# Attention's shared-out work dealt anew: one piece in the steps that weigh values and three in the others, and ten copies of weights in DRAM ahead of the attention instead of eight

## The chip, the cores and the metric

One NeuronCore of a Trainium2 chip runs the whole kernel. The metric is the device time of one execution in microseconds (us). Its engines work side by side, each through a queue of its own in a fixed order, and wait for each other through semaphores: PE (matmuls; PEld is its weight load), DVE (vector work), ACT (scalar activations and copies), POOL (GpSimd) and SP, which here only starts DMAs. POOL starts DMAs as well, among them all those that add into their destination.

## The reference, cut to what matters

One layer: attention over a sliding window, a residual, then a gated embedding. All in fp32.

```python
def swa_mixer(h, w_in, w_out, sinks, rel_bias):          # h: 512 x 2048
    q, k, v, gate = jnp.split(h @ w_in, ...)             # 32 q heads, 4 key/value heads, head size 64
    ...                                                  # blocks of 128; keys of this and the previous block
    scores = einsum(q, kb) * HD ** -0.5 + bias           # masked to a window of 128
    m = max(scores.max(-1), sink)
    e = exp(scores - m)
    probs = e / (e.sum(-1) + exp(sink - m))
    out = einsum(probs, vb)
    return (out * silu(gate)) @ w_out

def reference(...):
    x = x + swa_mixer(rmsnorm(x, norm_g), ...)
    x = x + (p @ ple_proj) * sigmoid(rmsnorm(x, ple_norm) @ ple_gate)
    return rmsnorm(x, final_g)
```

## The kernel before

Every fp32 matmul is three matmuls in a reduced format (`mm3`, L123 to L128): each operand is split into a high part and a rest, and high by high, high by rest and rest by high are added up in PSUM. The splitting is work for ACT (the high part is a cast) and DVE (the rest is a subtraction). For weights this is `W._make` (L104): it asks SP for the load after next, ACT makes `whi` (L109), DVE makes `wlo` (L110).

The stages follow each other on PE:

1. The first projections (k, v and two pieces of q) run while `first` is being loaded, up to about 71 us.
2. The other 30 pieces of the projections for q and the gate (`projections`, L856). A piece is 128 columns wide and takes 16 **k-steps** of three matmuls each. Half a piece needs one weight tile of 512 KB. The first 40 k-steps (L886) run alone, up to about 98 us.
3. The attention (loop L909) is woven into the rest of the projections: 64 **steps** i = 0 to 63, and three more in which its pipeline drains. Up to about 450 us. PE never has attention alone: each step holds 6 or 7 k-steps of projection.
4. The output projection and the embedding gate, in sub-products over sums of weights (seven instead of eight). The sums are made earlier: SP copies a block of weights from DRAM to DRAM (L693) and POOL adds another block onto the copy by a DMA (L695). There are 56 copies and as many adds. `sum_weights(n)` issues number n: an even n is a copy, an odd n the add for a copy that was issued seven numbers before.

One step i of the attention handles 32 queries of 8 heads. Several steps are in flight:

- `scores(i)`: PE multiplies q and k into `s` (L478; there is one such buffer). In the same step DVE adds the bias (`t`, L508) and takes the minimum (L511, into `sm`), ACT takes the exponential (L522) and, at the end of the step, DVE the reciprocal (L524). ACT scales the weights into `pr` (L533 to L537) in the next step.
- `turn(i-2)`: PE transposes `pr` into `pt` (L546), ACT casts the high part of `r` (L557), DVE subtracts the rest (L558); POOL masks a copy `own` (L565), of which ACT moves a half (L574).
- `weigh(i // 2 - 2)`, in even steps from 4 on: PE multiplies `r` by the values (L586, two matmuls, the second of which reads what L558 wrote) into `o`, one more matmul for `own` (L589), and then ACT copies halves of `o` into `tmp` (L598) and DVE adds them into `u` (L600).

PE's queue in a step begins with L586 (even steps), L546 and L478 and goes on with the step's k-steps. Between those, the rest is placed by hand in the loop L925: at each k-step n = 0 to 5 it calls parts of what is listed above and of these shared-out pieces:

- `W.todo` at n = 0: a weight tile's `whi` and `wlo`;
- `first_chores` at n = 0 and 4, up to step 5: splits of the values (`V`, L378, L379) and of their differences, and in steps 2 to 4 four DMAs each that spread the differences (L440);
- `chores`: three for each finished piece of projection. For q: `scaled` (DVE, L325), the high parts (ACT, L336), the rests (DVE, L334). For the gate: a product (DVE, L630), tanh (ACT, L631), a product (DVE, L624). A piece's PSUM bank is free after its third chore, and the piece after next is written into that bank;
- `idle`, if no chore is left: the splits of the next keys (L369, L367), the products of gate and output (L614).

Chores stand at n = 0, at n = 2 if more than one is left, and at n = 4, in every step alike. `weigh` goes on at n = 1 (L589) and n = 3 (L598, L600). At the end of a step come the copies and adds of weights that `sums_in(i)` lists. During the 40 k-steps ahead, eight copies are issued, at n = 6, 10, ..., 34 (L892); `SUMS_EARLY` counts the numbers that this covers.

Of the kernel before, what the change touches and what calls it, by code (L numbers as in the profile page):

```python
# [55 lines left out]
def trunk_kernel(ctx: ExitStack, tc: tile.TileContext, a: dict):  # L56
# [300 lines left out]
    def make_key(h):  # L357

        t, e = divmod(h, 2)
        k = K[h] = kvq.tile([P, S // QB, 2, QB], F32R, tag="k", name=f"k{h}", bufs=2)  # L360
        same = slice(64 * e, 64 * e + 64)

        def part(low):
            src = kt[t][same].rearrange("p (j k) -> p j k", k=QB)
            for o in (slice(0, 64), slice(64, 128)):
                if low:
                    nc.vector.tensor_sub(k[o, :, 1], src, k[same, :, 0].bitcast(F32))  # L367
                else:
                    nc.scalar.copy(k[o, :, 0], src)  # L369

        return partial_of(part, False), partial_of(part, True)
# [31 lines left out]
    for b in range(exact, BUCKETS):  # L403
        d = np.nonzero(bk == b)[0]
        if len(d):
            lo, n = P - 1 + int(d.min()), len(d)
# [35 lines left out]
    def first_chores(i, step):  # L442

        if step == 0 and i < NB - 1:
            make_diff(i + 1)
        if step and 1 <= i < NB:
            diffs[i][step - 1]()
        if step == 2 and 1 <= i - 1 < NB:
            spread_diff(i - 1)
        if step and 1 <= i - 2 < NB:  # L450
            split(V[i - 2], values[i - 2])[step - 1]()
# [87 lines left out]
    def turn(i):  # L539


        d, g = divmod(i, UNITS)
        pr = T.pop(i)
        pt = bank(f"pt{i}", "t")[:, :256]
        for u in range(2):
            nc.tensor.transpose(pt[:, u * P : (u + 1) * P], pr[:, u, :], ident)  # L546

        j, part = divmod(i, 2)
        if part == 0:
            own = None  # L550
            if g >= P // TQ:
                own = apool.tile([P, 2, S], F32R, tag="own", name=f"own{j}")
            PT[j] = apool.tile([P, 2, S], F32R, tag="r", name=f"r{j}"), own
        r, own = PT[j]
        rh, rl = (r[:, l].rearrange("p (h t u q) -> p t u h q", h=GROUP, t=2, u=2)[:, part] for l in range(2))
        src = pt.rearrange("p (u h q) -> p u h q", u=2, h=GROUP)
        nc.scalar.copy(rh, src)  # L557
        nc.vector.tensor_sub(rl, src, rh.bitcast(F32))  # L558
        yield
        b = j % 2  # L560
        flat = lambda v, rows: v[rows].rearrange("p l (h t q) -> p t (l h) q", h=GROUP, t=2)[:, part]
        if own is not None:
            rows = slice(0, P) if b else slice(0, HB)
            sign = -1 if b else 1
            nc.gpsimd.affine_select(  # L565
                out=flat(own, rows), in_=flat(r, rows).bitcast(F32), pattern=[[0, 2 * GROUP], [sign, TQ]],
                compare_op=ALU.is_ge, fill=0.0, base=(-HB - 1 if b else 0) + sign * part * TQ, channel_multiplier=-sign,
            )
        yield
        if own is not None:  # L570
            here, there = slice(HB, P), slice(0, HB)
            if not b:
                here, there = there, here
            nc.scalar.copy(flat(own, there)[:, :GROUP], flat(own, here)[:, GROUP:].bitcast(F32))  # L574

    def weigh(j):

        kv, m = divmod(j, S // HB)
        n, b = divmod(m, 2)
        r, own = PT.pop(j)  # L580
        if m == 0:
            U[kv] = apool.tile([P, 4, S], F32, tag="u", name=f"u{kv}", bufs=2)
        out = bank(f"o{j}", "o")
        first = V[0 if n == 0 else n - 1 + b][:, kv]
        for low in range(2):
            nc.tensor.matmul(out, first, r[:, low], start=low == 0, stop=own is None and low == 1)  # L586
        yield
        if own is not None:
            nc.tensor.matmul(  # L589
                out, DV[:, n - 1, b, kv * 2 * HD : (kv + 1) * 2 * HD], own[:, 0], start=False, stop=True  # L590
            )
        yield
        ops = out.rearrange("p (u e q) -> p u e q", u=4, e=2)
        dst = U[kv][:, :, m * HB : (m + 1) * HB]
        lower, upper = slice(0, 64), slice(64, 128)
        tmp = [apool.tile([P, 4, HB], F32, tag=f"tmp{e}", name=f"tmp{e}_{j}") for e in range(2)]
        for e, (o, x) in enumerate(((lower, upper), (upper, lower))):
            nc.scalar.copy(tmp[e][o], ops[x, :, e, :])  # L598
        for e, o in enumerate((lower, upper)):
            nc.vector.tensor_add(dst[o], ops[o, :, e, :], tmp[e][o])  # L600
        if m == S // HB - 1:
            for c in range(4 * kv, 4 * kv + 4):
                weighed.add(c)
                if c in open_gates:
                    idle.append(partial_of(gate_value, c))
# [3 lines left out]
    chores, idle = [], []  # L609
# [75 lines left out]
                copies.append((t, block(nm, *first, jj, m) if first else summed[nm, {6: 7, 4: 6}[p], jj, m]))  # L685
                adds.append((t, block(nm, *{7: (2, 2), 5: (1, 2), 6: (1, 1), 4: (2, 1)}[p], jj, m)))
    SUM_STEPS = 2 * len(copies) + 6
    SUMS_EARLY = 16

    def sum_weights(i):  # L690

        if i % 2 == 0 and i // 2 < len(copies):
            nc.sync.dma_start(*copies[i // 2])  # L693
        elif i % 2 == 1 and 0 <= i // 2 - 3 < len(adds):
            nc.gpsimd.dma_start(*adds[i // 2 - 3], accum_op=ALU.add, max_dma_last_dim=8192)  # L695
# [181 lines left out]
    def some(of, n=1):  # L877
        for _ in range(min(n, len(of))):
            of.pop(0)()
# [6 lines left out]
    for n in range(AHEAD):  # L886
        next(proj)
        if n % 4 == 3 and W.todo:
            W.todo.pop(0)()
        if n >= 2 * KC or n >= KC and n % 2:  # L890
            some(chores)
        if n >= 6 and n % 4 == 2 and n // 4 <= SUMS_EARLY // 2:  # L892
            sum_weights(2 * (n // 4 - 1))
    blocks = KVH * UNITS

    def sums_in(i):


        if i == 0:
            return ()  # L900
        if i < 4:
            return range(4 * i + 3, min(4 * i + 7, SUMS_EARLY), 2)
        n, of = SUM_STEPS - SUMS_EARLY, blocks - 4
        return range(SUMS_EARLY + (i - 4) * n // of, SUMS_EARLY + (i - 3) * n // of)

# [3 lines left out]
    for i in range(blocks + 3):  # L909

        before, softmax = softmax, scores(i) if i < blocks else iter(())
        turned = turn(i - 2) if 2 <= i < blocks + 2 else iter(())
        value = weigh(i // 2 - 2) if 4 <= i and i % 2 == 0 else iter(())
        next(value, None)
        next(turned, None)
        next(softmax, None)
        next(turned, None)
        next(before, None)
        next(softmax, None)
        first_chores(i, 0)  # L920
        if i in (6, 20, 36):
            idle.extend(make_key(1 + i // 16))
        todo = left // (blocks + 2 - i) if i < blocks + 2 else 0
        left -= todo
        for n in range(max(todo, 6)):  # L925
            if n < todo:
                next(proj)
            if n == 0:
                first_chores(i, 1)
                some(W.todo)  # L930
                some(chores or idle)
            elif n == 1:
                next(value, None)
            elif n == 2:
                if len(chores) > 1:
                    some(chores)
            elif n == 3:
                next(turned, None)
                next(value, None)
                next(softmax, None)  # L940
            elif n == 4:
                first_chores(i, 2)
                some(chores or idle)
            elif n == 5:
                next(softmax, None)
        if i < blocks:
            for n in sums_in(i):
                sum_weights(n)
# [434 lines left out]
    n = done[3]  # L1383
# [87 lines left out]
```

## Time and profile before

| | |
|---|---|
| runs, median | 797.51 us of 3 (797.0 to 798.45) |
| profiled execution | 797.58 us, of which 795.9 us are the span from its first to its last instruction |
| mean granted PE clock | 0.997 |
| PE busy | 783.1 us, 98% of the span |
| DVE, ACT, POOL busy | 590.7, 517.4, 141.7 us |
| HBM | 177.26 MB read, 62.97 MB written, 302 GB/s over the span |

The page gives for each engine how long it was busy. Since matmuls are pipelined, a record of one is longer (0.39 us) than the distance to the next start (0.23 us), so a short wait of PE hides in its busy time and is found in the starts of the timeline's rows instead. In the views, `[0.37 <-DVE sm L511]` behind an instruction is the idle time of its engine just before it and what ended that; a row of waits gives the total, the count and the longest, in us.

### The profile page before, as it was taken

The numbers are of one execution on the slowest core, as the hardware profiler recorded it, in microseconds if no ns is written. First come the engines' busy times: TensorE is split into PE (matmuls) and PEld (weight loads), VectorE is DVE, ScalarE is ACT, GpSimd is POOL, SyncE is SP. The second block draws the span as 40 slices with busy tenths as digits, with TensorE's granted clock in tenths as the row PEclk, the third lists the DMA queues.
The fourth block names the chain that finished last, engine by engine and source line by source line (L and its number), as shares of the span: only waits on it lengthen the run. The fifth ranks groups of instructions, "written<-read, shape, count | busy, mean of one in ns | idle before, by whom it ended". The sixth has DMA issues, their size and how long they took to land.

```text
span 795.9 us, 11177 instructions
## 1 busy us (share of the span) xinstructions
PE 783.1 (98%) x3658; PEld 649.4 (82%) x3658; DVE 590.7 (74%) x1171; ACT 517.4 (65%) x1131; POOL 141.7 (18%) x252
## 2 busy tenths in 40 slices
PE   9999999999999999999999999999999999999995
PEld 8888887878787888888888888888888888888885
DVE  4538567877887678776768799778867756988896
ACT  6635367876777667775767645456689656656765
POOL 0031122332243313341323100000000020210000
PEclk9999999999999999999999999999999999999998
DMA  9787779999899979889878498667873996796633
GB/s 349 231 227 262 204 181 283 296 237 285 242 254 260 249 227 249 240 235 274 241 201 181 126 367 317 224 208 233 286 243 127 348 201 201 162 230 208 190 106 106
DMA packets 44618, 184.87 MB, mean 232 GB/s; under 512 B 6720, under 2 KB 7232, under 8 KB 39440
## 3 DMA queue, kind: packets, MB, share of 16 engines
q1 hardware_dynamic: 36480, 142.94, 52.2%
q0 software_dynamic: 8080, 41.22, 27.4%
q8 instruction: 29, 0.48, 0.2%
q14 instruction: 29, 0.24, 0.1%
HBM read 177.26 MB, written 62.97 MB: 302 GB/s over the span
## 4 chain that ended last, share of the span: by engine, by line
PE 92%; DVE 4%; ACT 2%; DMA 1%; issue 1%; SPq 0%; ACTq 0%; DVEq 0%
PE gps L126 7%; PE gps L127 7%; PE gps L128 7%; PE qps L126 6%; PE qps L127 6%; PE qps L128 6%; PE g L128 5%; PE o L128 5%; PE g L127 5%; PE o L127 5%; PE o L126 5%; PE g L126 5%; PE vps L286 2%; PE s L478 2%; PE o L586 2%; PE pt L546 1%
## 5 line engine op out<-in xcount | busy, mean ns | idle before, releaser
L731 ACT CAST bhi<-braw 128x1024 fp32r<-128x1024 f32 x102 | 107.3, 1052 | 76.7 <-PE o L128 22.3
L732 DVE TENSOR_TENSOR blo<-braw,bhi 128x1024 fp32r<-128x1024 f32 x102 | 124.4, 1222 | 41.9 <-ACT bhi L731 41.5
L126 PE MATMUL gps<-xh,whi 128*128 128x512 f32 x256 | 100.5, 393 | 0.0
L127 PE MATMUL gps<-xl,whi 128*128 128x512 f32 x256 | 100.0, 391 | 0.0
L128 PE MATMUL gps<-xh,wlo 128*128 128x512 f32 x256 | 99.8, 390 | 0.0
L126 PE MATMUL qps<-xh,whi 128*128 128x512 f32 x224 | 87.6, 391 | 0.0
L127 PE MATMUL qps<-xl,whi 128*128 128x512 f32 x224 | 87.5, 391 | 0.0
L128 PE MATMUL qps<-xh,wlo 128*128 128x512 f32 x224 | 87.2, 389 | 0.0
L110 DVE TENSOR_TENSOR wlo<-wraw,whi 128x1024 fp32r<-128x1024 f32 x60 | 74.9, 1249 | 15.2 <-ACT whi L109 14.0
L126 PE MATMUL g<-bhi,fhg 128*128 128x512 f32 x192 | 75.1, 391 | 0.0
L126 PE MATMUL o<-bhi,fho 128*128 128x512 f32 x192 | 74.8, 390 | 0.0
L128 PE MATMUL g<-bhi,flg 128*128 128x512 f32 x192 | 74.8, 389 | 0.0
L128 PE MATMUL o<-bhi,flo 128*128 128x512 f32 x192 | 74.8, 389 | 0.0
L127 PE MATMUL g<-blo,fhg 128*128 128x512 f32 x192 | 74.7, 389 | 0.0
L127 PE MATMUL o<-blo,fho 128*128 128x512 f32 x192 | 74.7, 389 | 0.0
L109 ACT CAST whi<-wraw 128x1024 fp32r<-128x1024 f32 x60 | 62.3, 1040 | 11.7 <-issue 6.9
L565 POOL TENSOR_SCALAR_AFFINE_SELECT own<-r 64x512 fp32r<-64x512 f32 (+1 forms) x48 | 34.4, 716 | 163.1 <-DVE r L558 98.4
L493 POOL COPY t<-sinkb 128x2 f32<-128x2 f32 x64 | 41.3, 646 | 108.6 <-ACT pr L535 39.4
L558 DVE TENSOR_TENSOR r<-pt,r 128x256 fp32r<-128x256 f32 x64 | 27.1, 424 | 45.0 <-ACT r L557 44.2
L128 PEld LDWEIGHTS gps<-xh,wlo 128*128 128x128 f32 x256 | 48.1, 188 | 10.3
L126 PEld LDWEIGHTS gps<-xh,whi 128*128 128x128 f32 x256 | 48.1, 188 | 8.9
L127 PEld LDWEIGHTS gps<-xl,whi 128*128 128x128 f32 x256 | 48.1, 188 | 8.7
(230 smaller groups left out, 1730.2 us busy)
## 6 DMA issues: line engine op xcount, KB each, us to landing
w_out<-in_w_out POOLq DMA_DIRECT2D x32, 512.0 KB, 8.3
wraw<-in_w_gate_in SPq DMA_DIRECT2D x32, 512.0 KB, 7.1
braw<-w_out SPq DMA_DIRECT2D x32, 512.0 KB, 4.5
wraw<-in_w_q SPq DMA_DIRECT2D x28, 512.0 KB, 7.4
braw<-in_ple_gate SPq DMA_DIRECT2D x24, 512.0 KB, 4.3
braw<-in_w_out SPq DMA_DIRECT2D x22, 512.0 KB, 4.0
xw<-in_first SPq DMA_DIRECT2D x14, 640.5 KB, 6.4
w_out<-in_w_out SPq DMA_DIRECT2D x16, 512.0 KB, 8.8
```

Source lines behind the costliest of these rows:

```text
L109: nc.scalar.copy(hi, raw)
L110: nc.vector.tensor_sub(lo, raw, hi.bitcast(F32))
L126: nc.tensor.matmul(ps, sh, mh, start=first, stop=False, skip_group_check=more)
L127: nc.tensor.matmul(ps, sh, ml, start=False, stop=False, skip_group_check=more)
L128: nc.tensor.matmul(ps, sl, mh, start=False, stop=last, skip_group_check=more)
L286: nc.tensor.matmul(v_ps[t], h[:, c], part_of(high_at, 256, 512), start=f, stop=e, skip_group_check=True)
L478: nc.tensor.matmul(s_ps[:, u, : 2 * n], st, of_keys[:, first * 2 * QB : (first * QB + n) * 2], start=True, stop=True)
L493: nc.gpsimd.tensor_copy(two(0, W + W - 1 if late else W, 1), sinkb[:, d : d + 1].unsqueeze(1).to_broadcast([P, 2, 1]))
L558: nc.vector.tensor_sub(rl, src, rh.bitcast(F32))
L565: nc.gpsimd.affine_select(out=flat(own, rows), in_=flat(r, rows).bitcast(F32), pattern=[[0, 2 * GROUP], [sign, TQ]], compare_op=ALU.is_ge, ...
L731: nc.scalar.copy(hi, raw)
L732: nc.vector.tensor_sub(lo, raw, hi.bitcast(F32))
```

## The change

In even steps, those that weigh values, a chore (or an idle piece) is taken at n = 4 alone. In odd steps one is taken at n = 0, at n = 2 and at n = 4, and at n = 2 an idle piece may stand in for a chore. The third part of `weigh` (`tmp`, `u`) moves from n = 3 to n = 2 and so comes ahead of ACT's copy of `own` (L574). In the draining steps (i of 64 and more) n = 0 is kept. Ahead of the attention ten copies are issued, at n = 2, 6, ..., 38; steps 1 to 3 then issue two, two and three adds instead of two, two and one, and from step 4 on the list of copies and adds is two copies and two adds ahead of where it was.

```diff
-    SUMS_EARLY = 16
+    SUMS_EARLY = 20
...
-        if n >= 6 and n % 4 == 2 and n // 4 <= SUMS_EARLY // 2:
-            sum_weights(2 * (n // 4 - 1))
+        if n % 4 == 2 and n // 4 < SUMS_EARLY // 2:
+            sum_weights(2 * (n // 4))
...
         if i < 4:
-            return range(4 * i + 3, min(4 * i + 7, SUMS_EARLY), 2)
+            return range(4 * i + 3, 4 * i + 7 if i < 3 else SUMS_EARLY, 2)
...
             if n == 0:
                 first_chores(i, 1)
                 some(W.todo)
-                some(chores or idle)
+                if i % 2 or i >= blocks:
+                    some(chores or idle)
             elif n == 1:
                 next(value, None)
             elif n == 2:
-                if len(chores) > 1:
-                    some(chores)
+                next(value, None)
+                if i % 2:
+                    some(chores or idle)
             elif n == 3:
                 next(turned, None)
-                next(value, None)
                 next(softmax, None)
             elif n == 4:
                 first_chores(i, 2)
```

The order of PE's instructions is the same before and after. DVE's queue in step 4 and the beginning of step 5, where the number behind a name is that of its buffer; before:

```order
L110 TENSOR_TENSOR wlo_1255<-wraw_1193,whi_1254 128x1024
L325 SCALAR_TENSOR_TENSOR qps_1087<-qps_1087,rb 128x512
L600 TENSOR_TENSOR u_1224<-o_1225,tmp_0_1270 64x4x64
L600 TENSOR_TENSOR u_1224<-o_1225,tmp_0_1271 64x4x64
L379 TENSOR_TENSOR V_732<-misc,V_732 128x4x64
L334 TENSOR_TENSOR q_1086<-qps_1087,q_1086 64x32x16 x2
L524 RECIPROCAL sm_1242<-sm_1242 128x2
L558 TENSOR_TENSOR r_1231<-pt_1293,r_1231 128x2x8x16
L508 TENSOR_TENSOR t_1301<-s_1298,bias_839 128x2x144
```

and now:

```order
L110 TENSOR_TENSOR wlo_1259<-wraw_1195,whi_1258 128x1024
L600 TENSOR_TENSOR u_1228<-o_1229,tmp_0_1268 64x4x64
L600 TENSOR_TENSOR u_1228<-o_1229,tmp_0_1269 64x4x64
L379 TENSOR_TENSOR V_732<-misc,V_732 128x4x64
L325 SCALAR_TENSOR_TENSOR qps_1089<-qps_1089,rb 128x512
L524 RECIPROCAL sm_1246<-sm_1246 128x2
L558 TENSOR_TENSOR r_1235<-pt_1293,r_1235 128x2x8x16
L508 TENSOR_TENSOR t_1301<-s_1298,bias_839 128x2x144
```

Of the q piece's chores only `scaled` (L325) is left in step 4, behind `u`; the rests (L334) have gone to step 5, behind its L508 and L511. The same happens in steps 12, 20 and 28 (and 42, 58), where all three chores of a q or gate piece stood in one even step.

ACT's queue at the same place, before:

```order
L109 CAST whi_1254<-wraw_1193 128x1024
L336 CAST q_1086<-qps_1087 64x32x16 x2
L598 COPY tmp_0_1270<-o_1225 64x256
L598 COPY tmp_0_1271<-o_1225 64x256
L522 ACTIVATE t_1237,sm_1242<-t_1237,sm_1242 128x129 x2
L557 CAST r_1231<-pt_1293 128x2x8x16
```

and now:

```order
L109 CAST whi_1258<-wraw_1195 128x1024
L598 COPY tmp_0_1268<-o_1229 64x256
L598 COPY tmp_0_1269<-o_1229 64x256
L522 ACTIVATE t_1241,sm_1246<-t_1241,sm_1246 128x129 x2
L557 CAST r_1235<-pt_1293 128x2x8x16
```

ACT's casts of q (L336) no longer stand between the weight's cast and `tmp`; they follow in step 5, behind that step's `pr`.

POOL's queue at the end of step 3 and in step 4 (L493 and L496 prepare `t`, L695 are the adds), before:

```order
L496 MEMSET t_1177 128x16
L695 DMA w_out_0_2_786<-in_w_out 64x2048 [waits DMAHW1_49]
L493 COPY t_1237<-sinkb 128x2 [waits DVE_49,Activation_49]
L493 COPY t_1301<-sinkb 128x2 [waits DVE_49,Activation_49,Pool_49]
L695 DMA w_out_0_3_787<-in_w_out 64x2048 [waits DMAHW2_49,DMASW1_49]
```

and now:

```order
L496 MEMSET t_1179 128x16
L695 DMA w_out_0_2_786<-in_w_out 64x2048 [waits DMAHW0_49]
L695 DMA w_out_0_3_787<-in_w_out 64x2048 [waits DMAHW2_49,DMASW1_49]
L695 DMA w_out_1_0_788<-in_w_out 64x2048 [waits DMAHW3_49]
L493 COPY t_1241<-sinkb 128x2 [waits DVE_49,Activation_49]
```

Step 3 starts three adds in a row where it started one; the two others came later, behind the preparations of steps 5 and 6.

## Prediction

> **What bounds the kernel now.** I read the page first: is PE the bound, and is there anything left of it to win?
>
> ```profile
> span 795.9 us, 11177 instructions
> ...
> PE 783.1 (98%) x3658; PEld 649.4 (82%) x3658; DVE 590.7 (74%) x1171; ACT 517.4 (65%) x1131; POOL 141.7 (18%) x252
> ```
>
> PE is busy for 98% of the span. PE's instructions and their order do not change, so the change can gain only where PE waits. Next, the views of the waits, of PE's weight load and of PE:
>
> ```profile
> PEld o L586 <- DVE r L558: 3.4, 4, 1.4
> ```
>
> ```profile
> PE s L478 <- DVE sm L511: 1.5, 4, 0.4
> ```
>
> Four times PE waits for the rest of `r`, and four times for the minimum in `sm`. Since a short wait hides in a matmul's record, I take its price from starts in PE's timeline: from the first L586 of a step to its L478 are two value matmuls and two transposes. First the four places, then the same sequence without a wait, at the top of step 32:
>
> ```profile
> 125.53 0.40 PE L586 MATMUL o<-r,V 128*128 128x512 f32 x1
> ...
> 128.09 0.50 PE L478 MATMUL s<-k,q 128*128 128x288 f32 x2 [0.37 <-DVE sm L511]
> ...
> 166.79 0.40 PE L586 MATMUL o<-r,V 128*128 128x512 f32 x1
> ...
> 168.61 0.50 PE L478 MATMUL s<-k,q 128*128 128x288 f32 x2 [0.37 <-DVE sm L511]
> ...
> 207.17 0.81 PE L586 MATMUL o<-r,V 128*128 128x512 f32 x2
> ...
> 208.63 0.50 PE L478 MATMUL s<-k,q 128*128 128x288 f32 x2 [0.37 <-DVE sm L511]
> ...
> 247.33 0.40 PE L586 MATMUL o<-r,V 128*128 128x512 f32 x1
> ...
> 249.40 0.50 PE L478 MATMUL s<-k,q 128*128 128x288 f32 x2 [0.37 <-DVE sm L511]
> ...
> 260.00 0.63 PE L586 MATMUL o<-r,V 128*128 128x512 f32 x2
> ...
> 260.61 0.39 PE L478 MATMUL s<-k,q 128*128 128x32 f32 x2
> ```
>
> The sequence takes 2.56, 1.82, 1.46 and 2.07 us at the four places (steps 6, 14, 22 and 30) and 0.61 us at the fifth. The waits are worth 1.95 + 1.21 + 0.85 + 1.46 = 5.47 us. All other even steps show about 0.6 there.
>
> Why is DVE late just there? The chain that ended last, in order of time (start, length, what; its longest pieces, the steps of under 0.3 us left out by the view itself), from the weight load of step 4 on:
>
> ```profile
> 107.84 10.75 DMA wraw<-in_w_gate_in
> 118.61 1.06 ACT whi L109
> 119.70 1.23 DVE wlo L110
> 120.92 0.62 DVE qps L325
> 121.57 0.58 ACT q L336
> 122.16 0.58 ACT q L336
> 122.75 0.37 ACT tmp L598
> 123.13 0.37 ACT tmp L598
> 123.53 0.42 DVE u L600
> 123.96 0.43 DVE u L600
> 124.40 0.33 DVE V L379
> 124.84 0.69 DVE q L334
> 125.54 0.69 DVE q L334
> 126.46 0.42 DVE r L558
> 126.88 0.38 DVE t L508
> 127.28 0.37 DVE t L511
> 127.66 0.28 DVE t L511
> ```
>
> In step 4 a q piece's three chores and the third part of `weigh` form one chain that changes engine four times: DVE scales q, ACT casts it, ACT then copies `o`, DVE adds that into `u`, DVE splits q. Only behind that stand the reciprocal of step 4 and the L558 and L511 of step 5, which PE wants at 125.53. PE, whose k-steps need none of this, has run a whole step ahead by then. The other three places are the same pattern (steps 12, 20, 28).
>
> **The four waits: from the chain to the new order.** In step 4 ACT now goes from the weight's cast (ends 119.67) to `tmp` (2 × 0.37, to 120.43), the exponential and the high part of `r`; DVE from `wlo` (ends 120.92) to `u` (0.43 + 0.43, to 121.80), `V` (0.44 to the next start, 122.25), `scaled` (0.62 to 0.70, 122.95), the reciprocal (0.23 from the end of the rests, 126.23, to L558; 123.18) and L558 (0.42, 123.60). The exponential's length is in ACT's timeline:
>
> ```profile
> 123.52 0.40 ACT L522 ACTIVATE t<-t,sm 128x129 f32<-128x129 f32 x1
> ...
> 124.31 0.35 ACT L557 CAST r<-pt 128x256 fp32r<-128x256 f32 x1
> ```
>
> It takes 0.79 us, so it ends at about 121.2 and the cast L557 at 121.6, ahead of DVE's reciprocal: neither holds DVE. L511 ends 1.49 us after the start of L558 (126.46 to 127.66 + 0.28 in the chain), so at 124.67. PE asks for L558 from 125.53 on and would issue L478 at 125.53 + 0.61 = 126.14. Both are ready 1.5 to 2 us earlier, and the whole 1.95 us falls away. At the other three places the chain from the end of `wlo` loses the same members, about 3.3 us of 7.0, against waits of 0.85 to 1.46 us, so they fall too: −5.47 us.
>
> **The pieces that move to odd steps.** ACT's casts of q (2 × 0.58) and DVE's rests (2 × 0.69) now stand in step 5, behind its L511 and ahead of its exponential. Step 5 has no `u` and no `tmp`. Continuing the sum: `pr` on ACT to about 124.3, the casts to 125.5, the exponential to 126.3; on DVE the rests to 126.9, `V` to 127.3, the reciprocal to 127.5, L558 of step 6 to 128.0, L511 to 129.0. PE wants the latter in step 7, which begins some 4.6 us after 126.14 (six k-steps of 0.68 us, row below, and 0.5 us for scores and transposes): margin 1.7 us. What is late next is step 10. The next keys' split goes from steps 6 and 8 (n = 0) to n = 4 of steps 7 and 8; carried on with the same durations, L511 of step 9 is done about 0.1 us before PE wants it. Before, that place was near its edge as well (DVE's and PE's timeline):
>
> ```profile
> 147.25 0.08 DVE L511 DVE_READ_ACCUMULATOR2_ANT sm<- 128x1 f32 x1
> ```
>
> ```profile
> 147.62 0.51 PE L478 MATMUL s<-k,q 128*128 128x288 f32 x2
> ```
>
> From 147.33 to 147.62 are 0.29 us. I price it at 0, with 0.5 us as the upper bound.
>
> **A model of the new order inside the trace.** Piece q 11 ends in step 30 after n = 2, so only `scaled` falls into step 30 already, behind `u`, and the casts and rests into step 31. The next L558 in DVE's timeline:
>
> ```profile
> 255.58 0.42 DVE L558 TENSOR_TENSOR r<-pt,r 128x256 fp32r<-128x256 f32 x1
> ```
>
> It ends at 256.00, and PE's L586 at 260.00 (the row above) takes the result without a wait, 4.0 us later. That is the row nearest to the new even step.
>
> **The copies and adds.** Two more copies go out ahead of the attention. SP issues its copies well ahead of PE, and none of the waits listed for PE or PEld is one for weights in that stage; I price them at 0. Cover gone, it would be a late weight load, as in the next case. The two adds brought forward start right behind step 3's:
>
> ```profile
> 108.72 0.77 POOL L695 DMA_DIRECT2D w_out<-in_w_out  x1 [0.23 <-issue]
> ```
>
> An add goes through POOL's queue of the DMA engines (packets, MB, share of 16 engines' span):
>
> ```profile
> q0 software_dynamic: 8080, 41.22, 27.4%
> ```
>
> POOL spends 2 × 0.8 us on issuing, from 109.5 to 111.1; its next work, step 4's `t`, waits for that step's buffer anyway, since ACT's `pr` of step 2 must be done with it: 0. But the weight load of the chain is under way from 107.84 to 118.59, and ACT waits for it ahead of `tmp`. An add of 0.52 MB takes 27.4% × 795.9 / 41.22 × 0.52 = 2.8 us of all DMA engines. If POOL's queue works its adds off one after the other, the two stand behind the one of 108.72 and touch the load little: 0. If they run beside it, the load is up to 5.5 us later. [...] No row here shows two adds in parallel, so I take 0 and keep the lateness as a rival.
>
> **Sum.** 797.58 us of the profiled execution (795.9 span and 1.7 around it) − 5.47 = 792.1 us. The profiled execution stands 0.07 us above the median of 797.51, so nothing is to be corrected.
>
> **The rivals.**
>
> *A, the first wait stays in part, by a late weight load.* In step 4 everything hangs on ACT's `whi`, and the margin before L478 is 126.14 − 124.67 = 1.5 us. A load later by L leaves L − 1.5 of wait. With one add in the way (2.8) that is 1.3 us: 793.4. With both (5.5) it is 4.0 instead of 1.95: 797.58 − 3.52 + 2.05 = 796.1. Against it: the load's price of 10.75 us was paid already with POOL's adds under way.
>
> *B, the wait only changes its step.* The work per two steps is the same, and an odd step may now hold three pieces and a weight. If odd steps then push the next L511 past PE, the four waits return as waits of L478 in steps 7, 15, 23, 31: 797.5. For it: DVE is busy for 74% overall and the margins of step 7 to 10 are 0.1 to 1.7 us. Against: the model in steps 30 and 31, and that the odd step lacks `u` and `tmp` (1.6 us).
>
> *C, slower: PE waits for a PSUM bank.* With one chore per even step, a piece's third chore comes later. Following the loop, 14 pieces now have 6 or 7 k-steps between their third chore and the start of the piece after next, where none had fewer than 8 before. A k-step lasts 0.68 us:
>
> ```profile
> 175.15 0.39 PE L126 MATMUL gps<-xh,whi 128*128 128x512 f32 x1
> ...
> 175.83 0.39 PE L126 MATMUL gps<-xh,whi 128*128 128x512 f32 x1
> ```
>
> So DVE must stay less than 4.1 us behind PE there. The tightest that I worked is q 5: its rests end at about 126.9, and PE needs the bank at step 6, n = 4, 126.14 + 0.35 + 4 × 0.68 = 129.2, margin 2.3 us. If DVE were 3.3 us later than in my sum, each of 14 places would wait about 1 us: 792.1 + 14 = 806. It ends on the slow side from a lag of 2.7 us (14 × 0.4 = 5.6 us) on. DVE did lag that much before, but behind the very chain that is cut.
>
> That the change does not do what it says is excluded by the order rows: the three chores are out of the even steps.
>
> **How the numbers follow.** All four waits gone, 80%; A 9%, all of it faster; B 6%; C 5%. The forecast is 792.1. Its own range is 791.3 to 793.2: the 0.5 us of step 10 above, and below and above the scatter of the runs shown (0.5 below and 0.9 above their median). A adds up to about one more wait of 1.3 to 2 us: the range is 791.2 to 794.6, without A's upper half, B and C. A measurement of this kernel can tell about 0.2%, 1.6 us, from no change. Faster by more than that: the forecast and nearly all of A, 0.88; the same: B and the last of A, 0.07; slower: C, 0.05.
>
> **What would show it.** Right: L586 to L478 takes about 0.6 us in every even step; the row of L586 waiting for L558 is gone from the waits; the last L586 of the attention (near 450 us before) starts about 5.5 us earlier, and all behind it keeps its length. A would show as idle time of ACT's `whi` behind a DMA at 118 to 122 us; B as waits of L478 for L511 in odd steps; C as waits at the first L126 of a piece for L334, L624 or L631. If the starts of the attention's steps are earlier but the end is not, the stage behind it waits for weights, which nothing here shows. A gain under 2 us would make the prediction wrong in its mechanism.

## The result, and the profile after

The changed kernel takes 795.43 us (median of 20 runs, 793.61 to 797.87), the kernel before 797.92 us in the 20 runs beside them (797.0 to 800.15). The ratio is 0.9969, with a 95% interval of 0.9961 to 0.9977. So the change gains 2.5 us; I had forecast 792.1 us, 5.4 us of gain, and no time above 794.6. The direction was right and the size was not: 3.3 us are missing. The profiled execution took 796.87 us. One run in all, of the last experiment (873.35 us at a mean clock of 0.849), fell into a slower state of the chip and is left out of every comparison.

The span is 795.2 us, against 795.9 before. On the page of the changed kernel PE is the bound as before:

```profile
PE 784.2 (99%) x3658; PEld 651.3 (82%) x3658; DVE 590.6 (74%) x1171; ACT 517.1 (65%) x1131; POOL 143.5 (18%) x252
```

PE's timeline at the four places whose waits were to go, from L586 to L478 in steps 6, 14, 22 and 30 (columns: start, length, instruction, and in brackets the idle time before it):

```profile
126.41 0.50 PE L586 MATMUL o<-r,V 128*128 128x512 f32 x1
128.03 0.50 PE L586 MATMUL o<-r,V 128*128 128x512 f32 x1 [1.13 <-DVE r L558]
...
129.19 0.50 PE L478 MATMUL s<-k,q 128*128 128x288 f32 x2 [0.24 <-DVE sm L511]
...
169.51 0.63 PE L586 MATMUL o<-r,V 128*128 128x512 f32 x2
...
170.12 0.51 PE L478 MATMUL s<-k,q 128*128 128x288 f32 x2
...
208.69 0.63 PE L586 MATMUL o<-r,V 128*128 128x512 f32 x2
...
209.29 0.51 PE L478 MATMUL s<-k,q 128*128 128x288 f32 x2
...
247.97 0.63 PE L586 MATMUL o<-r,V 128*128 128x512 f32 x2
...
248.58 0.51 PE L478 MATMUL s<-k,q 128*128 128x288 f32 x2
```

Three of the four sequences now take 0.61, 0.60 and 0.61 us. The first takes 2.78 us, more than the 2.56 before. The chain that ended last shows why, from the same weight load on:

```profile
108.46 14.88 DMA wraw<-in_w_gate_in
...
123.37 1.06 ACT whi L109
...
124.45 1.22 DVE wlo L110
125.68 0.33 DVE u L600
...
126.90 0.70 DVE qps L325
...
127.66 0.32 DVE r L558
```

Behind `wlo` the chain is as short as I worked it out: `u`, `V`, `scaled`, L558. But the load takes 14.88 us instead of 10.75 and lands at 123.34 instead of 118.59. What the new order saved, the load ate up.

The second surprise stands behind that wait. The same window of both kernels in the table of windows (start and end, then busy time and count of PE, PEld, DVE, ACT and POOL, the granted clock of PE, DMA share, GB/s), before and after:

```profile
125.00:135.00 10.00, 8.61 (x41) 6.67 (x40) 7.68 (x23) 7.62 (x23) 2.74 (x4) 1.00 0.90 286
```

```profile
125.00:135.00 10.00, 8.57 (x29) 6.07 (x29) 8.90 (x26) 7.84 (x25) 2.75 (x4) 0.83 1.03 349
```

The granted clock falls to 0.83 in the mean of these 10 us. The same table gives 0.50 from 130 to 132 us (a half clock), and in PE's timeline the starts are 0.43 us apart from 129.80 to 133.17, where they are 0.23 us otherwise:

```profile
130.65 0.63 PE L126 MATMUL qps<-xh,whi 128*128 128x512 f32 x1
131.08 0.63 PE L127 MATMUL qps<-xl,whi 128*128 128x512 f32 x1
```

Eight starts in 3.37 us in place of 8 x 0.23 = 1.84: 1.5 us lost. The profiled executions add up so. The attention's first L586 (timelines, before and after) is 0.66 us later ahead of all this, and its last one 0.70 us earlier:

```profile
115.87 0.63 PE L586 MATMUL o<-r,V 128*128 128x512 f32 x2
...
449.41 0.63 PE L586 MATMUL o<-r,V 128*128 128x512 f32 x2
```

```profile
116.53 0.63 PE L586 MATMUL o<-r,V 128*128 128x512 f32 x2
...
448.71 0.63 PE L586 MATMUL o<-r,V 128*128 128x512 f32 x2
```

Between them lie the three waits that went (-3.52), the first place (it begins 0.22 us later still and takes 0.22 us more) and the half clock (+1.5): 0.66 + 0.44 + 1.5 - 3.52 = -0.9, against -0.70.

The profiled execution is not a typical one, though. Five of the 20 runs, the profiled one among them, have a mean clock of 0.994 or 0.995 and take 796.17 to 797.87 us. Fourteen lie at 793.61 to 795.97 us with 0.996 to 0.998, and one at 796.99 us with 0.996. So, as far as the mean clock tells, the median run has no half clock, and the 3.3 us that it lacks are not all explained by this profile. The run with the copies back, below, shows what can stand in its place.

### The profile page after: what moved, and what is told of

Its sections match the earlier page's. It is cut to its first block, busy times and chain, and to the rows that moved or that the text cites. A ratio compares the mean times of both kernels' runs of the same rounds, so it can differ in the third digit from the quotient of the medians.

```text
span 795.2 us, 11179 instructions
## 1 busy us (share of the span) xinstructions
PE 784.2 (99%) x3658; PEld 651.3 (82%) x3658; DVE 590.6 (74%) x1171; ACT 517.1 (65%) x1131; POOL 143.5 (18%) x252
## 4 chain that ended last, share of the span: by engine, by line
PE 96%; DMA 2%; DVE 1%; ACT 0%; SPq 0%; issue 0%; ACTq 0%; DVEq 0%
PE gps L126 7%; PE gps L127 7%; PE gps L128 7%; PE qps L126 7%; PE qps L127 7%; PE qps L128 6%; PE g L128 5%; PE o L127 5%; PE g L126 5%; PE o L128 5%; PE o L126 5%; PE g L127 5%; PE s L478 2%; DMA wraw<-in_w_gate_in 2%; PE vps L286 2%; PE o L586 2%
## 5 line engine op out<-in xcount | busy, mean ns | idle before, releaser
L557 ACT CAST r<-pt 128x256 fp32r<-128x256 f32 x64 | 23.8, 372 | 72.1 <-PE pt L546 72.0
L558 DVE TENSOR_TENSOR r<-pt,r 128x256 fp32r<-128x256 f32 x64 | 27.1, 423 | 56.9 <-ACT r L557 56.6
L493 POOL COPY t<-sinkb 128x2 f32<-128x2 f32 x64 | 42.5, 664 | 105.2 <-ACT pr L535 40.2
```

What stands on the lines that cost most here:

```text
L493: nc.gpsimd.tensor_copy(two(0, W + W - 1 if late else W, 1), sinkb[:, d : d + 1].unsqueeze(1).to_broadcast([P, 2, 1]))
```

## The experiments

Theory 1: the adds that step 3 now starts together make the weight load of step 4 late, and all of the shortfall follows from that. Theory 2: the two extra copies ahead make it late. Theory 3: the new order does not free the first place. The kernel before took 797.45 us beside the first four experiments, 797.72 beside the next four and 797.85 beside the last three.

**The order of the pieces alone.** The changed loop, with the copies and adds as before the change:

```diff
-    SUMS_EARLY = 20
+    SUMS_EARLY = 16
...
-        if n % 4 == 2 and n // 4 < SUMS_EARLY // 2:
-            sum_weights(2 * (n // 4))
+        if n >= 6 and n % 4 == 2 and n // 4 <= SUMS_EARLY // 2:
+            sum_weights(2 * (n // 4 - 1))
...
-            return range(4 * i + 3, 4 * i + 7 if i < 3 else SUMS_EARLY, 2)
+            return range(4 * i + 3, min(4 * i + 7, SUMS_EARLY), 2)
```

> The new dealing of the pieces, with the copies and adds of weights where they were before (eight copies ahead, one add in step 3). Theory 1, two early adds make the weight load of step 4 late: with them gone that load takes about 10.75 us again as before the change (14.88 after it), ACT no longer idles 4.69 us ahead of its cast, all four places show 0.6 us from L586 to L478, and the granted clock stays at 1.00 from 125 to 135 us (0.83 after the change). Time 792.1 to 792.9. Theory 2, two early copies make it late: the same, since they are gone too. Theory 3, the new dealing itself does not free the first place: the first place still shows some 2.5 us, the time is 794.4 or more.

Measured: 792.71 us, ratio 0.9937 (0.9923 to 0.9951). ACT's cast of that weight in the timeline:

```profile
119.22 1.05 ACT L109 CAST whi<-wraw 128x1024 fp32r<-128x1024 f32 x1 [0.69 <-DMA wraw<-in_w_gate_in]
```

ACT idles 0.69 us for the load, not 4.69, and no start of PE in the attention is more than 0.3 us late. Theory 3 is out.

**The copies and adds alone.** The old loop with the new code of copies and adds:

```diff
-                if i % 2 or i >= blocks:
-                    some(chores or idle)
+                some(chores or idle)
...
-                next(value, None)
-                if i % 2:
-                    some(chores or idle)
+                if len(chores) > 1:
+                    some(chores)
             elif n == 3:
                 next(turned, None)
+                next(value, None)
```

> The order of the pieces as before the change, with ten copies ahead and three adds in step 3 as after it. Theories 1 and 2: the load lands some 4.1 us later, and since in the old order the whole chain of step 4 hangs on it, the first wait grows from 1.95 to about 6 us; the nine slow matmuls cost up to 1.7 us more: 797.6 + 4.1 to 5.8 = 801.7 to 803.4. My prediction's step, that copies and adds take nothing, and theory 3: 797.5.

Measured: 803.27 us, ratio 1.007 (1.0054 to 1.0085): slower than before by 5.8 us. PE's timeline:

```profile
129.36 0.73 PE L586 MATMUL o<-r,V 128*128 128x512 f32 x1 [3.15 <-ACT r L557]
131.59 0.80 PE L586 MATMUL o<-r,V 128*128 128x512 f32 x1 [1.49 <-DVE r L558]
```

PE waits twice, together 4.6 us by the brackets. By the starts it is more: the last projection matmul before starts at 125.83, so L586 is 129.36 - 126.06 = 3.3 us late, and L478 follows at 132.74, 3.38 us behind it in place of 0.61. That is 6.1 us, where the kernel before waited 1.95, and the granted clock is 0.50 from 130 to 136 us. The half of the change that I had priced at nothing costs more than the whole change gains.

**Which of the two: the adds, or the copies.** Both from the changed kernel. First the adds go back to their old places, and the ten early copies stay; then the copies go back (eight ahead), and the three adds in step 3 stay (`listed` gives the old list for 16, the new one for 20):

```diff
     def sums_in(i):
+        of_copies, of_adds = listed(i, 20), listed(i, 16)
+        return sorted([n for n in of_copies if n % 2 == 0] + [n for n in of_adds if n % 2])
```

```diff
-        if n % 4 == 2 and n // 4 < SUMS_EARLY // 2:
-            sum_weights(2 * (n // 4))
+        if n >= 6 and n % 4 == 2 and n // 4 <= 8:
+            sum_weights(2 * (n // 4 - 1))
...
     def sums_in(i):
+        of_copies, of_adds = listed(i, 16), listed(i, 20)
+        return sorted([n for n in of_copies if n % 2 == 0] + [n for n in of_adds if n % 2])
```

> The changed kernel with its ten early copies kept, but each add at the place that it had before the change (one in step 3). Theory 1 (the adds): the load of step 4 lands after about 10.75 us, no wait at the first place, clock 1.00 there: 792.1 to 792.9. Theory 2 (the copies): load about 14.9 us, the wait stays: like the changed kernel, 795.4. Theory 3: like the changed kernel.

> The changed kernel with its three adds in step 3 kept, but eight copies ahead of the attention, each at its place before the change. Theory 1 (the adds): like the changed kernel, 794.5 to 796.5, load of step 4 about 14.9 us. Theory 2 (the copies): load about 10.75 us and 792.1 to 792.9. Theory 3: like the changed kernel.

Measured: adds back 792.17 us, 0.9932 (0.992 to 0.9945); copies back 795.52 us, 0.9972 (0.9963 to 0.9981), like the changed kernel. ACT's cast in the first and in the second:

```profile
118.20 1.05 ACT L109 CAST whi<-wraw 128x1024 fp32r<-128x1024 f32 x1 [0.37 <-DMA wraw<-in_w_gate_in]
```

```profile
123.32 1.05 ACT L109 CAST whi<-wraw 128x1024 fp32r<-128x1024 f32 x1 [5.02 <-DMA wraw<-in_w_gate_in]
```

Theory 2 is out: the two copies cost nothing, the two adds 3.3 us. With the adds back all four waits are gone, PE's last L586 is 5.7 us earlier than before (449.41), and the time is the one forecast:

```profile
443.69 0.63 PE L586 MATMUL o<-r,V 128*128 128x512 f32 x2
```

The profiled run with the copies back (796.38 us) shows one thing more. Its clock in 125 to 135 us is 1.00, and it still reaches the same time, because PE waits again in steps 9 and 10. PE's and ACT's timeline there:

```profile
143.47 0.38 PE L546 MATMUL pt<-ident,pr 128*128 128x128 f32 x2
144.21 0.50 PE L478 MATMUL s<-k,q 128*128 128x288 f32 x2 [0.36 <-DVE sm L511]
...
149.11 0.38 PE L546 MATMUL pt<-ident,pr 128*128 128x128 f32 x2
149.61 0.50 PE L478 MATMUL s<-k,q 128*128 128x288 f32 x2
```

```profile
140.83 1.25 ACT L369 CAST k<-kt 64x512 fp32r<-64x512 f32 x2
142.10 0.37 ACT L557 CAST r<-pt 128x256 fp32r<-128x256 f32 x1
```

From L546 to L478 are 0.74 and 0.50 us where 0.14 is normal (169.98 to 170.12 in the changed kernel): 0.6 + 0.4 = 1.0 us. ACT and DVE still carry the lateness of step 4, and the next keys' cast (L369, 1.25 us), an idle piece, stands ahead of the L557 that PE needs. In the changed kernel's profiled run they are just as late: there that L557 begins at 142.15, against 142.10 here. But PE, held back by the half clock, comes to the L478 behind it only at 145.31, against 144.21 here. So there PE lost 1.5 us on its clock and nothing in steps 9 and 10. In both profiles the late load is thus paid for at a second place.

**The load asked for earlier.** The changed kernel with its three adds, but every weight tile is requested one tile earlier, in `W._make`:

```diff
-            self.load(min(i + 2, len(self.srcs)))
+            self.load(min(i + 3, len(self.srcs)))
```

> The changed kernel, three adds in step 3 kept, but every weight tile is asked for one tile earlier, so that the load of step 4 stands on SP's queue ahead of the four spreads (L440) and is issued near 101 us, as soon as its buffer is free, in place of 108.46. Theory 1 (the adds cost only because that load is beside them): it lands before the three adds start, all four places show 0.6 us, 792.0 to 793.0. Rival (the adds hurt in step 3 by something else, the load being only one sign of it): 795 to 796. A second rival, that the earlier loads now hold up SP's copies and spreads: a wait at another place, 793 to 796.

Measured: 792.15 us, 0.9932 (0.992 to 0.9944). The load is issued at 100.42 and lands at 104.11, ahead of all adds of step 3, and ACT no longer waits for it:

```profile
117.90 1.05 ACT L109 CAST whi<-wraw 128x1024 fp32r<-128x1024 f32 x1
```

With no urgent load beside them, the three adds in step 3 cost nothing in this run (792.15 against 792.17 with the adds back). This version and the one with the adds back beat both kernels.

**Two adds in place of three.** The variant with the adds back, with 18 in place of 16:

```diff
-        of_copies, of_adds = listed(i, 20), listed(i, 16)
+        of_copies, of_adds = listed(i, 20), listed(i, 18)
```

> The changed kernel's copies, with two adds in step 3 (one in the first variant of this kind, 792.17; three in the changed kernel, 795.43). If each add beside the load costs it the same, (14.88 - 10.51) / 2 = 2.2 us, the load takes about 12.7 us; of that lateness about 2 us are covered, so 792.2 to 793.0. If two adds already take the load to its full lateness of about 14.9 us: 795.4. If the second add finds the load nearly done and only the third counts: load about 10.5 to 11 us, 792.2.

Measured: 793.59 us, 0.9952 (0.994 to 0.9964).

```profile
121.36 1.05 ACT L109 CAST whi<-wraw 128x1024 fp32r<-128x1024 f32 x1 [2.82 <-DMA wraw<-in_w_gate_in]
```

The load takes 13.0 us, 2.5 us more than with one add, and 1.9 us less than with three: the second and the third add cost the load about the same here. The two adds land at about 118.4 and 121.4, and the load with the second, at 121.34. The time is above what I expected from the first place alone. PE's timeline has a wait of 0.5 us there (0.14 normal from L546 to L478) and again 0.55 us in step 9; 0.4 us come in step 10:

```profile
126.50 0.44 PE L546 MATMUL pt<-ident,pr 128*128 128x128 f32 x2
127.18 0.51 PE L478 MATMUL s<-k,q 128*128 128x288 f32 x2 [0.23 <-DVE sm L511]
...
141.55 0.38 PE L546 MATMUL pt<-ident,pr 128*128 128x128 f32 x2
142.24 0.50 PE L478 MATMUL s<-k,q 128*128 128x288 f32 x2 [0.31 <-DVE sm L511]
```

Together 1.45 us, and 793.59 - 792.17 = 1.42 (the profiled run itself took 794.21 us).

**Copies in place of the two adds.** The changed kernel; the second and third DMA of POOL in step 3 write without adding, which leaves the addition out of two blocks of summed weights:

```diff
-            nc.gpsimd.dma_start(*adds[i // 2 - 3], accum_op=ALU.add, max_dma_last_dim=8192)
+            nc.gpsimd.dma_start(*adds[i // 2 - 3], **({} if i in (17, 19) else dict(accum_op=ALU.add)), max_dma_last_dim=8192)
```

> The changed kernel, in which the second and third DMA of POOL in step 3 (numbers 17 and 19) write their block without adding it: the same bytes written from the same source through the same queue, without the destination being read. This leaves out the addition in two blocks of summed weights. If the load is late because the adds' bytes share the 16 DMA engines with it, and the reading of the destination is a part of those bytes, the load is less late than the changed kernel's 14.88 us: 12 to 13.5 us and 792.8 to 794.5. If only the number and place of the transfers counts: about 14.9 us, 795.4. If a plain copy takes no share of the load's: 10.5 us, 792.2.

Measured: 792.75 us, 0.9934 (0.9921 to 0.9947); the load takes 12.9 us. The profiled run, at 794.09 us the longest of the six, waits about 1.4 us in steps 6, 9 and 10; the other five (792.34 to 792.82) can have waited little, but they have no profile. Two plain copies cost the load 12.9 - 10.5 = 2.4 us, and the adding another 2.0 us up to 14.88: here the adding, not only the transfer, made the load late. The queues' shares of the DMA engines from 118 to 120 us (packets, MB, share of 16 engines) in the changed kernel, in this one, and with the adds back, where POOL's queue is empty then:

```profile
q0 software_dynamic: 47, 0.35, 84.5%
q1 hardware_dynamic: 49, 0.14, 19.0%
```

```profile
q0 software_dynamic: 93, 0.63, 76.0%
q1 hardware_dynamic: 91, 0.21, 26.7%
```

```profile
q1 hardware_dynamic: 246, 0.61, 105.0%
```

In these 2 us a packet of POOL's queue (q0) took 0.845 x 16 x 2 us / 47 = 0.58 us in the changed kernel and 0.26 us in the run with the two copies; one of SP's queue (q1, which carries the load) took 0.12 us in the changed kernel. In the changed kernel, with adds open from 118 to 124 us, SP's queue had 19.0, 16.2 and 18.5% of the engines in the three stretches of 2 us, and POOL's 84.5, 86.7 and 92.7%; with the adds back SP's had all of them from 118 to 120 us (105.0%). The packets of the two queues were about as many in the first two views (47 and 49, 93 and 91) but not everywhere (36 of POOL's and 81 of SP's from 114 to 116 us in the changed kernel), so these counts do not show by what rule the engines divide their time.

**Which half of the new order frees the waits.** Both from the variant with the adds back. In the first, `weigh` stays at n = 3; in the second only `weigh` moves, and the chores stand in every step as before:

```diff
             elif n == 2:
-                next(value, None)
                 if i % 2:
                     some(chores or idle)
             elif n == 3:
                 next(turned, None)
+                next(value, None)
```

```diff
-                if i % 2 or i >= blocks:
-                    some(chores or idle)
+                some(chores or idle)
...
-                if i % 2:
-                    some(chores or idle)
+                if len(chores) > 1:
+                    some(chores)
```

> The variant with the adds put back (792.17), but the third part of weigh stays at n = 3 as before the change; only the chores are dealt anew. My theory: the q piece's chores were what made the chain of step 4 long; without them nothing is gained by the place of weigh, and all four places stay at 0.6 us: 792.0 to 792.8. Rival (the place of weigh does it): the four waits come back in good part, 795 to 797.

> The same variant, but the chores stand in every step as before the change (n = 0, n = 2 if more than one is left, n = 4); only the third part of weigh moves to n = 2, ahead of that chore. By my theory's own sum the move alone lets ACT copy o before it casts q, so the chain of step 4 no longer changes engine four times: scaled 0.62, u 0.87, V 0.44, the rests 1.39, the reciprocal 0.23 and L558 0.42 behind the end of wlo at 120.92 make 124.9, and L511 ends at about 126.0 where PE wants it at 126.14. So the move alone takes nearly all: 792.2 to 793.4. Rival (the length of DVE's work in the even step counts, not the changes of engine): a half or more of the four waits stays, 794.5 to 796.

Measured: chores alone 792.55 us, 0.993 (0.9917 to 0.9943); `weigh` alone 792.57 us, 0.9928 (0.9915 to 0.9942). Either half does it alone. DVE's timeline of the second in step 4, with all of the q piece's work still there:

```profile
121.26 0.69 DVE L325 SCALAR_TENSOR_TENSOR qps<-qps,rb 128x512 f32<-128x512 f32 x1
121.86 0.85 DVE L600 TENSOR_TENSOR u<-o,tmp 64x256 f32<-64x256 f32 x2
122.72 0.42 DVE L379 TENSOR_TENSOR V<-misc,V 128x256 fp32r<-128x256 f32 x1
123.19 1.39 DVE L334 TENSOR_TENSOR q<-qps,q 64x512 fp32r<-64x512 f32 x2
...
124.81 0.42 DVE L558 TENSOR_TENSOR r<-pt,r 128x256 fp32r<-128x256 f32 x1
...
126.22 0.08 DVE L511 DVE_READ_ACCUMULATOR2_ANT sm<- 128x1 f32 x1
```

DVE does the same work without a gap, where before it stood still for 2.0 us (121.54 to 123.53 in the chain before) while ACT cast q and then copied `o`. So with the amount of work in the even step unchanged, it is enough to take this change of engine out of the chain: the standing still, not the work by itself, cost the four waits. This version has the smaller margin: L511 ends at 126.30 and PE's L478 starts at 126.64. With the chores dealt anew and the adds back it is 123.87 against 125.93.

**A wait by itself, and the clock.** The variant with the adds back; DVE writes the rests of `r` of step 5 eleven or fifteen times, which holds up PE at step 6 and nothing in its queue is changed:

```diff
-        nc.vector.tensor_sub(rl, src, rh.bitcast(F32))
+        [nc.vector.tensor_sub(rl, src, rh.bitcast(F32)) for _ in range(11 if i == 3 else 1)]
```

> The variant with the adds put back (792.17), in which DVE writes the rests of r of step 5 (L558) eleven times instead of once, the same values each time: 10 x 0.43 us = 4.3 us more on DVE, of which about 2.1 us are covered, so PE waits about 2.2 us at step 6 and nothing else is changed in PE's queue. If such a wait is enough to halve the granted clock, as in the profiled run of the changed kernel, some runs show a clock of 0.994 to 0.995 and 1.6 us more: 794.4 to 797. [...]

> As the kernel before it, with L558 of step 5 written fifteen times: 14 x 0.43 = 6.0 us more on DVE, about 3.9 us of wait for PE at step 6. By both views of the clock some or all runs should now show the half clock: 796.1 without it, up to 797.8 with it. If no run shows it, a wait of this length is not what halves the clock.

Measured: eleven times 796.83 us, 0.9981 (0.997 to 0.9991); fifteen times 799.4 us, 1.0017 (1.0008 to 1.0026). PE's timeline, eleven and fifteen times:

```profile
126.21 0.40 PE L586 MATMUL o<-r,V 128*128 128x512 f32 x1
128.24 0.50 PE L586 MATMUL o<-r,V 128*128 128x512 f32 x1 [1.63 <-DVE r L558]
...
129.40 0.74 PE L478 MATMUL s<-k,q 128*128 128x288 f32 x2 [0.43 <-DVE sm L511]
```

```profile
125.55 0.40 PE L586 MATMUL o<-r,V 128*128 128x512 f32 x1
130.03 0.79 PE L586 MATMUL o<-r,V 128*128 128x512 f32 x1 [4.09 <-DVE r L558]
...
131.19 0.82 PE L478 MATMUL s<-k,q 128*128 128x288 f32 x2
```

The waits are 3.19 - 0.61 = 2.6 and 5.64 - 0.61 = 5.0 us, somewhat longer than expected. The runs of the first fall into two groups: four at 794.77 to 795.11 us, which is 792.17 + 2.6, with a mean clock of 0.996 to 0.998, and seven at 796.6 to 797.64 with 0.994 to 0.996, 2.1 us more in the mean. Of the second's eleven runs that are compared, one has 797.93 us and a clock of 0.996 and ten have 798.16 to 800.33 with 0.991 to 0.995. So, going by times and mean clocks (only one run of each has a profile, with a granted clock of 0.83 and 0.67 from 125 to 135 us, against 1.00 with the adds back), the half clock came in seven of the eleven runs with a wait of 2.6 us, and in ten of the eleven with one of 5.0 us. No run shows a length of wait from which the clock must fall.

## Why the prediction was wrong

- **The four waits, 5.47 us: right.** Without the early adds the change gains 5.3 us (792.17 against 797.45), at 0.1 us from the forecast, and all four places show 0.6 us. The sum along the chain held too: L511 was to end 1.47 us ahead of PE and ended 2.06 us ahead. I had put the gain on both halves of the new order together; each does it alone.
- **The odd steps and step 10, 0 with 0.5 us as upper bound: right by itself, and too little in company.** With the adds back PE waits at none of them. With the load late, steps 9 and 10 take another 1.0 us. I had found this place to be the tightest and did not carry it into rival A.
- **Two more copies ahead, 0: right** (795.52 against 795.43 with the adds early; 792.17 against 792.71 with the adds at their old places).
- **The two adds brought forward, 0: this step failed.** They cost 3.3 us (795.43 against 792.17). I wrote: "If POOL's queue works its adds off one after the other, the two stand behind the one of 108.72 and touch the load little: 0." The first half is true. In the changed kernel the three adds were issued at 109.38, 110.21 and 110.72 and landed at 118.34, 121.32 and 124.12, 3 us apart. What did not follow is the second half. The load stands in another queue, SP's, behind the spreads issued before it (the last of them landed at 117.60, before at 116.70), and while adds were open in POOL's queue, SP's had 16.2 to 19.0% of the engines from 118 to 124 us. Before, POOL's queue was done with step 2's adds at about 113.3 and with step 3's one add at 118.14, and the load landed right behind, at 118.59; now two more adds were open behind that one, and the load landed at 123.34. I took 0 because no row showed two adds in parallel. But the three adds landed one after the other and the load was late all the same; what counted was that adds were open beside it, and the trace of before did show that: adds open beside the load until 118.14, and 10.75 us for it, where a weight load of the same 512 KB took 3.7 us with neither adds nor spreads open, in the kernel before (issued at 97.7) and in the run with the load asked for earlier (100.42 to 104.11).
- **Rival A, 9%: right in its mechanism.** "A load later by L leaves L - 1.5 of wait." L was 14.88 - 10.75 = 4.1 us (that the load was also issued 0.6 us later counts for nothing, since PE was as much later), the margin came out at 2.1 us, and the first wait at 2.78 - 0.61 = 2.2 us. Rival A's price with both adds was 796.1 us, by a load 5.5 us late. That it came near the profiled time rests on terms that it lacked, steps 9 and 10 or the half clock, in place of a lateness that was too large.
- **The half clock: not foreseen at all.** It takes 1.5 us by the starts of the profile, and 2.1 us by the two groups of runs with eleven writes.
- **Rivals B and C: false.** No wait moved to the odd steps while the load was on time, and none was for a PSUM bank.

## What to carry to other kernels

When a transfer is moved, look at what urgent load is under way on any other queue at its new place, and ask what share of the DMA engines the load keeps; that transfers of one queue follow each other said nothing here about a load in another queue (adds that landed 3 us apart, and a load of 14.88 us in place of 10.75). Where a chain through several engines makes the bound wait, first look for an order with fewer changes of engine: moving one copy ahead of two casts was worth as much here as dealing out all of the chores anew (792.57 and 792.55 us). A margin that is worked out for one change alone is to be worked out again with every other part's lateness in it.

## What the runs showed of the hardware

- With adds open in POOL's queue from 118 to 124 us of the changed kernel, SP's queue had 16.2 to 19.0% of the DMA engines and POOL's 84.5 to 92.7%; with the adds back, SP's had 105.0% from 118 to 120 us. From 118 to 120 us of the changed kernel a packet of POOL's queue took 0.58 us and one of SP's 0.12 us. With plain copies in place of two of the three adds, a packet of POOL's queue took 0.26 us, and the load 12.9 us against 14.88.
- In the changed kernel's profiled run the granted clock was 0.50 from 130 to 132 us, behind idle stretches of PE of 1.13 and 0.24 us with a value matmul and two transposes between; the starts were 0.43 us apart for 3.4 us (129.80 to 133.17). With eleven writes, where the profile has 1.63 and 0.43 us of idle time there, the clock was 0.83 from 125 to 135 us, and by their times seven of the eleven runs had the half clock. With the copies back the same sequence took 2.79 us, against 2.78, and the clock was 1.00. So the length of the wait alone did not decide it; what else did, no run shows.
- The half clock took the place of later waits in one profile: the changed kernel's profiled run lost 1.5 us on its clock and did not have the waits of steps 9 and 10, which took 1.0 us with the copies back.
